# A two-layer hybrid trunk on one core: ScalarE copies, a group of weight rests and the last layer's end put in another order

## The chip, the cores and the metric

The kernel runs on one core of a Trainium2 chip. A core has TensorE (PE, with its weight loads shown as PEld), VectorE (DVE), ScalarE (ACT), GpSimd (POOL) and SyncE (SP, which here only issues DMAs). Each engine takes its instructions strictly in program order. The metric is device microseconds of one execution of the whole program. Three runs of the kernel before gave 1378.09 us in the median (1377.64 to 1379.01).

## The reference

```python
for i in range(DEPTH):                       # 2 layers; x is 256 x 1024, float32
    u = x @ w_in[i]                          # 512 pool columns, 512 values, 512 gates
    y_pool = pool_mixer(u_pool, ...)         # trailing-window means, grouped projection
    y_conv = conformer_conv(u_val, u_gate, ...)   # v = a*sigmoid(gate); 31 causal taps; norm; silu; @ w_pw
    x = layer_norm(ALPHA * x + concat([y_pool, y_conv]) @ w_out[i], ...)
    if i % 2 == 0: f = swiglu(x, ...)        # dense, 2816 hidden columns
    else:          f = moe_swiglu(x, ...)    # 8 experts of 3584 hidden columns, the top 2 of each token
    x = layer_norm(ALPHA * x + f, ...)
    x = x + sigmoid(x @ ple_gate_w[i]) * (p[i] @ ple_w[i])
```

## The kernel before

Tokens stand in two halves of 128, called h = 0 and 1. For every projection the activations are transposed (token columns, 8 tiles k of 128 features) and are the stationary operand; a weight tile of up to 512 columns streams past them into one PSUM bank.

Products are made in float32 precision out of a reduced format (fp32r). Activations and weights are each split into a high part H (a copy rounded to fp32r by ACT, L143 for weights and L317 for activations) and a rest L, the difference, by DVE (L158 and L318). One product of a k tile is then three matmuls: xH by wH (L344), xH by wL (L348) and xL by wH (L349). Weights named in `DIRECT` are not split: one full float32 matmul (L341) takes the unsplit activations `f` and the weight as it was loaded. Narrow experts (64 places) hold H and L of their tokens side by side and need two matmuls (L344, L346) and a product with the matrix `shift` that adds the two halves (L1045).

All weights pass through one ring of 19 slots of 8 KB per partition ("w"). `Weights` holds them in the order of use. `prepare(name, n)` and `get(i)` call `advance`, which emits the cast on ACT and the rest on DVE for each weight item up to the wanted one, and goes on ahead of need up to the item `W.cap`, as long as no more than `W.hl` slots hold split weights. Where such a call stands in the code is where its casts and rests stand in ACT's and DVE's queues. The same calls issue the loads on SP, a number of slots ahead. The code's order is the engines' order; nothing reorders it.

The places that the change touches, in order of time:

- Start: `shift` is filled from the identity in the constants `con` (L299), then ACT loads its sigmoid table (L313), then the two halves of x and the first weights are split.
- `mixer`: gate and value projections of the convolution group, `gate(b, h)` and `value(b, h)`, with 256 columns each; `diagonals(b)` writes 16 diagonal matrices on ACT (L497), which `conv(b)` multiplies on PE (L503). In layer 1 `late` transposes and splits the second half of x, which the layer before left over; it runs in the middle of `value(0, 0)`.
- `moe`, before the experts: norm, then for each half transposes and splits, the product with expert 0's first weights w1 (`p1`), the routing (logits `lg`, mask `msk`, positions, `select`), and the split of the second weights `w3e0_0` (L848).
- `experts`: 56 blocks of 512 hidden columns, each up by w1 and w3, down by w2; the last four blocks are narrow.
- The end of `moe` and `embed_gate`: `last(h)` adds half h of the last expert's output (`ps_sc`), the norm follows (`norm_begin`, `norm_apply`), `to_xT` transposes and splits 512 features at a time, `emit` makes products of the embedding (`ps_ple`), and the gate projection (`ps_gate`, weights `gate0`, `gate1`, each 512 columns) is combined and stored by 512 or, at the very end, 256 columns.

`acc` takes one of four PSUM banks in turn and `mmt` one of the four others. `keep_warm(n)` makes n products that nobody reads. POOL computes the inverse root of the norm.

Of the kernel before, what the change touches and what calls it, by code (L numbers as in the profile page):

```python
# [17 lines left out]
P = 128  # L18
# [3 lines left out]
KD = D // P  # L22
# [12 lines left out]
ND = len(DENSE_CHUNKS)  # L35
SLOTS = 19
HL_START, HL_PRE, HL_FIRST, HL_SECOND, HL_MOE = 8, 12, 8, 6, 10
DIRECT = ("pw0", "pw1", "wo00", "wo01")
DT = 23
MORE_AT = 53  # L40
WARM = 16
# [4 lines left out]
WU_EARLY = 2  # L46
# [5 lines left out]
EM = 3, 0  # L52
GL = 6
END = ((0, 256), (256, 256))
# [139 lines left out]
def trunk(ctx: ExitStack, tc: tile.TileContext, a: dict, out: bass.AP):  # L194
    nc = tc.nc
# [9 lines left out]
    def acc(name, k=None):  # L205

        if k is None:
            k = at[0] % 4
            at[0] += 1
        return pacc.tile([P, 512], F32, tag=f"acc{k}", name=name)  # L210
# [85 lines left out]
    H = P // 2  # L296
    shift = cp.tile([P, P], F32R, name="shift")
    nc.gpsimd.memset(shift[:, H:].bitcast(F32), 0.0)
    nc.scalar.copy(shift[:, :H], ident[:, H:])  # L299
    wr = tl("m2", [KD, NE])  # L300
    nc.gpsimd.dma_start(wr, a["router"])
    neghalf = cp.tile([P, 1], F32, name="neghalf")
# [19 lines left out]
    def new_xT(f=None):  # L322
        return [Split(tl(f"xH{h}", [KD, P], F32R), tl(f"xL{h}", [KD, P], F32R), None if f is None else f[:, h])
                for h in range(2)]
# [10 lines left out]
    def to_xT(dst, src, c):  # L335

        split_into(dst[:, 4 * c:4 * c + 4, :], transposes(src[:, c * 512:(c + 1) * 512], 4))
# [124 lines left out]
    def mixer(l, xT, xr, late, loads):  # L462
# [31 lines left out]
        def diagonals(b):  # L494
            for i in range(2):
                for k in range(TAPS - DT):
                    nc.scalar.activation(dg[:, i * 8 + k], ident, AF.Copy, scale=weight(2 * b + i, DT + k))  # L497
# [8 lines left out]
        def gate(b, h, between=None):  # L506
            pg = acc("ps_g")
            proj(W.names[f"wg{b}{l}"], pg, xT[h], free=h == 1, also=lambda k: k == GB and between and between())
            nc.scalar.activation(vb[b][h], pg[:, :256], AF.Sigmoid)

        def value(b, h, between=None):
            pv = acc("ps_v")
            proj(W.names[f"wv{b}{l}"], pv, xT[h], free=h == 1, also=lambda k: k == GB and between and between())
            nc.vector.tensor_mul(vb[b][h], pv[:, :256], vb[b][h])
# [3 lines left out]
            copy(vT[b][:, :, 32 + h * P:32 + (h + 1) * P], transposes(vb[b][h], 2))  # L518

        W.temps = TEMPS_MIX  # L520
        diagonals(0)

        gate(0, 0)
        if l == 0:
            gate(0, 1)
            value(0, 0)
        else:
            value(0, 0, late)
            gate(0, 1)
        W.prepare(f"wg1{l}")  # L530
        value(0, 1, lambda: turn(0, 0))
# [306 lines left out]
    def moe(l, xr, gb1, mix, project):  # L838
# [6 lines left out]
        sc = norm_begin(xr[1], mix[1], lambda: to_xT(xT[0], xr[0], 1))  # L845
        for c in range(2):
            norm_apply(gb1, xr[1], sc, c)
        W.prepare("w3e0_0", None)  # L848
        table(AF.Sigmoid)

        p1 = [acc("p1") for _ in range(2)]
# [13 lines left out]
        to_xT(xT[1], xr[1], 0)  # L865
        router(0, range(KD))
        to_xT(xT[1], xr[1], 1)
        W.hl = HL_SECOND
        routed = []

# [45 lines left out]
        last = experts(ranks, gates, xr, yacc, (selT, gsl, xg), lambda: hidden(g, 512, 0),  # L916
                       lambda: over(ci, beyond, gate, xr, yacc), end)
        gb, (ple, emit, _) = late["gains"], late["ple"]
        xT2 = new_xT()
        table(AF.Sigmoid)  # L920
        last(0)
        sc = [norm_begin(yacc[0], None)]
        W.prepare(f"gate0{l}", 2)
        emit(EM[0])
        for c in range(2):
            norm_apply(gb, yacc[0], sc[0], c)
        to_xT(xT2[0], yacc[0], 0)
        emit(EM[1])
        last(1)
        W.prepare(f"gate0{l}", 3)  # L930
        to_xT(xT2[0], yacc[0], 1)
        emit(4 - EM[0] - EM[1])
        sc.append(norm_begin(yacc[1], None))
        W.prepare(f"gate0{l}", 4)
        for c in range(2):
            norm_apply(gb, yacc[1], sc[1], c)
        W.prepare(f"gate1{l}", None)
        return xT2, yacc, lambda c: to_xT(xT2[1], yacc[1], c), ple

    def route(lg):  # L940
# [96 lines left out]
    def experts(ranks, gates, xr, yacc, nxt, first, more, end):  # L1037
# [9 lines left out]
        for i, (e, c) in enumerate(BLOCKS):  # L1047
# [11 lines left out]
            p1 = mmt("p1")  # L1059
            final = i == len(BLOCKS) - 1  # L1060
            if final:
                W.cap = W.names[f"w2e{prev[0]}_{prev[1]}"][1]
            both(f"w1e{e}_{c}", [p1], [xg])
            if made is not None:
                prev[3] = made()
# [23 lines left out]
            if final:  # L1089
                down(ids[:1], paccs, pgT, pc == 0, False, True)  # L1090
                if narrow:
                    fold(p3, lo[:, 1])
                    g = glu(s_, p3, 512, par, gsl)
                W.cap = W.names[f"w2e{e}_{c}"][-1] + 1
                W.hl = HL_PRE
                down(ids[1:], paccs, pgT, False, pc == FE - 1, True, 2)
            else:
                down(ids, paccs, pgT, pc == 0, pc == FE - 1, True)
                if narrow:
                    fold(p3, lo[:, 1])  # L1100
                    g = glu(s_, p3, 512, par, gsl)
# [36 lines left out]
    def embed_gate(l, xT, late, xr, ple, last):  # L1138

        xTn = None if last else new_xT()  # L1140

        def combine(h, c, ps, i=0, n=512):

            sg = tl(f"s{h}", [512])[:, i:i + n]
            cs = slice(c * 512 + i, c * 512 + i + n)
            nc.scalar.activation(sg, ps[:, :n], AF.Sigmoid)  # L1146
            nc.vector.tensor_mul(sg, sg, ple[:, h, cs])  # L1147
            nc.vector.tensor_add(xr[h][:, cs], sg, xr[h][:, cs])  # L1148
            if last:
                nc.sync.dma_start(out[h * P:(h + 1) * P, cs], xr[h][:, cs])  # L1150

        for c in range(2):
            ids = W.names[f"gate{c}{l}"]
            for h in range(2):
                if last and c and h:

                    for i, n in END:
                        ps = acc("ps_gate")
                        for k in range(KD):
                            mm(ps[:, :n], xT[h][:, k, :], W.get(ids[k // 2]), (ALL, k % 2, slice(i, i + n)),  # L1160
                               k == 0, k == KD - 1)
                        combine(h, c, ps, i, n)
                    continue
                ps = acc("ps_gate")
                proj(ids[:2], ps, xT[h], last=False, free=h == 1)
                if c == h == 0 and not last:
                    late()
                    W.prepare(f"gate1{l}")
                if c and h == 0 and not last:
                    to_xT(xTn[0], xr[0], 0)  # L1170

                def between(k):
                    if c == h == 0 and last and k == GL:
                        late(0)
                    if c and h and k == GK:
                        to_xT(xTn[0], xr[0], 1)
                proj(ids[2:], ps, xT[h], 4, first=False, free=h == 1, also=between)
                if c == h == 0 and last:
                    late(1)
                combine(h, c, ps)  # L1180
                if c and h == 0 and not last:
                    W.prepare(f"wg1{l + 1}")
            if c == 0 and not last:
                W.prepare(f"wv0{l + 1}")
        if not last:
            W.temps = TEMPS_MIX
            W.hl = HL_PRE
            W.prepare(f"wv1{l + 1}", None)
            W.prepare(f"wu{l + 1}", WU_EARLY)
        return xTn, lambda: [to_xT(xTn[1], xr[1], c) for c in range(2)]  # L1190

    warm = tl("cat", [512], mybir.dt.bfloat16)
# [4 lines left out]
    for h in range(2):  # L1197
        split_into(xT[h], xF[:, h])
        W.prepare("wg00" if h == 0 else "wv00")
    late = lambda: None  # L1200
    loads = mixer_loads(0)
    for l in range(L):
# [100 lines left out]
```

## Time and profile before

| what | value |
|---|---|
| median of three runs | 1378.09 us (1377.64 to 1379.01) |
| profiled execution, its own time | 1376.18 us |
| its span, first to last instruction | 1374.4 us |
| PE busy, matmuls | 1317.2 us (96%) x6314 |
| DVE busy | 1173.5 us (85%) |
| ACT busy | 921.8 us (67%) |
| rests of weights on DVE (L158) | 460, 891.8 us |
| casts of weights on ACT (L143) | 460, 750.8 us |
| read from HBM | 430.85 MB, 314 GB/s over the span |
| mean granted TensorE clock | 0.986 of full |

The span begins with the first instruction; the execution's own time is 1.8 us longer, and the median of the three runs another 1.9 us. PE's shares are high nearly everywhere, so a change in the order of work is read at the places where PE stands idle and at what ends that wait, with the name after the arrow in a row of the trace.

### The profile page before, as it was taken

What the parts mean: (1) busy time and instruction counts of PE and PEld (TensorE: products, weight loads), DVE (VectorE), ACT (ScalarE), POOL (GpSimd) and SP (SyncE); (2) the same over time, 40 slices, a digit from 0 to 9 for tenths busy, and PEclk for the clock granted to TensorE, in tenths of its full rate; (3) what the DMA queues carried; (4) which work ended last, traced back from release to release, by engine and by line L of the source; (5) the groups of instructions that cost most, each with busy time, mean ns of one, the idle gap of its engine ahead of it and who ended that gap; (6) DMA issues with size and microseconds to landing.
All of it is one profiled execution on the core that took longest, in us unless ns stands there. A gap on an engine that the chain in (4) does not pass through costs nothing. (4 is left out here: it accounts for less than half of the span.)

```text
span 1374.4 us, 17077 instructions
## 1 busy us (share of the span) xinstructions
PE 1317.2 (96%) x6314; PEld 1084.8 (79%) x6314; DVE 1173.5 (85%) x1102; ACT 921.8 (67%) x863; POOL 26.0 (2%) x33
## 2 busy tenths in 40 slices
PE   6999999999999999999999999999999999999777
PEld 5868888888967788878888878888887888888556
DVE  3987755466786989999999999999999999999885
ACT  5534544336333768887887887888787888898662
POOL 0000000010000200000000000000000000000000
PEclk8999999999998999999999999999999999999999
DMA  9436555526554499999999999999999999999850
GB/s 375 157 139 217 214 191 195 191 91 242 210 218 157 180 341 405 420 418 359 422 420 394 410 421 379 397 421 405 396 420 404 379 419 414 388 377 420 353 213 31
DMA packets 62172, 433.09 MB, mean 315 GB/s; under 512 B 6960, under 2 KB 7472, under 8 KB 11008
## 3 DMA queue, kind: packets, MB, share of 16 engines
q1 hardware_dynamic: 60336, 425.60, 78.5%
q0 software_dynamic: 1168, 4.23, 0.9%
q10 hardware_dynamic: 576, 2.10, 0.4%
q8 instruction: 51, 0.84, 0.2%
q14 instruction: 41, 0.34, 0.1%
HBM read 430.85 MB, written 1.05 MB: 314 GB/s over the span
## 5 line engine op out<-in xcount | busy, mean ns | idle before, releaser
L158 DVE TENSOR_TENSOR w<-w 128x2048 fp32r<-128x2048 f32 (+1 forms) x460 | 891.8, 1987 | 56.4 <-ACT w L143 49.8
L143 ACT CAST w<-w 128x2048 fp32r<-128x2048 f32 (+1 forms) x460 | 750.8, 1672 | 134.7 <-PE p L348 42.7
L344 PE MATMUL p<-w,xH 128*128 128x512 f32 (+1 forms) x1096 | 433.5, 396 | 9.5 <-ACT w L143 6.6
L349 PE MATMUL p<-w,xL 128*128 128x512 f32 (+1 forms) x648 | 250.9, 387 | 1.3 <-DVE xL L318 1.3
L348 PE MATMUL p<-w,xH 128*128 128x512 f32 (+1 forms) x648 | 250.2, 386 | 0.4 <-DVE w L158 0.4
L344 PEld LDWEIGHTS p<-w,xH 128*128 128x128 f32 x1096 | 207.6, 189 | 51.8 <-ACT w L143 7.0
L344 PE MATMUL y<-w,gH 128*128 128x512 f32 x448 | 176.2, 393 | 3.1 <-DVE gH L379 2.4
L346 PE MATMUL p<-w,xH 128*128 128x512 f32 x448 | 175.8, 392 | 0.0
L349 PEld LDWEIGHTS p<-w,xL 128*128 128x128 f32 x648 | 122.4, 189 | 26.7 <-DVE xL L318 1.8
L348 PEld LDWEIGHTS p<-w,xH 128*128 128x128 f32 x648 | 122.6, 189 | 24.6 <-DVE w L158 1.3
L344 PEld LDWEIGHTS y<-w,gH 128*128 128x128 f32 x448 | 84.6, 189 | 21.6 <-DVE gH L379 3.1
L346 PEld LDWEIGHTS p<-w,xH 128*128 128x128 f32 x448 | 85.0, 190 | 16.9
L346 PE MATMUL y<-w,gH 128*128 128x512 f32 x224 | 88.3, 394 | 1.9 <-DVE w L158 1.9
L349 PE MATMUL y<-w,gL 128*128 128x512 f32 x224 | 87.4, 390 | 1.2 <-DVE gL L318 1.2
L348 PE MATMUL y<-w,gH 128*128 128x512 f32 x224 | 87.3, 390 | 0.0
L484 DVE SCALAR_TENSOR_TENSOR yc<-w,vec,yc 128x256 f32<-128x256 f32 x176 | 70.4, 478 | 0.0
L645 ACT ACTIVATE s<-p 128x512 f32<-128x512 f32 (+1 forms) x69 | 41.2, 599 | 27.7 <-PE p L349 27.7
L318 DVE TENSOR_TENSOR gL<-tr,gH 128x512 fp32r<-128x512 f32 x38 | 25.7, 684 | 32.7 <-ACT gH L317 32.7
L346 PEld LDWEIGHTS y<-w,gH 128*128 128x128 f32 x224 | 42.6, 190 | 11.0 <-DVE w L158 2.3
L317 ACT CAST gH<-tr 128x512 fp32r<-128x512 f32 x38 | 21.9, 587 | 43.6 <-PE tr L332 43.0
L349 PEld LDWEIGHTS y<-w,gL 128*128 128x128 f32 x224 | 42.0, 188 | 10.4 <-DVE gL L318 1.6
L348 PEld LDWEIGHTS y<-w,gH 128*128 128x128 f32 x224 | 42.1, 188 | 9.0
(223 smaller groups left out, 1415.9 us busy)
## 6 DMA issues: line engine op xcount, KB each, us to landing
w<-in_exp_w SPq DMA_DIRECT2D x336, 1024.0 KB, 8.7
w<-in_dense_w SPq DMA_DIRECT2D x33, 1024.0 KB, 5.0
w<-in_w_out SPq DMA_DIRECT2D x8, 1024.0 KB, 6.4
w<-in_ple_gate_w SPq DMA_DIRECT2D x8, 1024.0 KB, 5.1
w<-in_w_gv SPq DMA_DIRECT2D x6, 1024.0 KB, 7.2
w<-in_w_u SPq DMA_DIRECT2D x4, 1024.0 KB, 10.2
w<-in_w_gv SPq DMA_DIRECT2D x4, 512.0 KB, 7.3
w<-in_w_small SPq DMA_DIRECT2D x2, 1024.0 KB, 9.1
```

What stands on the lines that cost most here:

```text
L143: nc.scalar.copy(h, w)
L158: engine.tensor_tensor(l, w, h.bitcast(F32), op=ALU.subtract)
L317: nc.scalar.copy(dst.h, src)
L318: nc.vector.tensor_sub(dst.l, src, dst.h.bitcast(F32))
L344: nc.tensor.matmul(ps, x.h, wh, start=start, stop=False)
L346: nc.tensor.matmul(ps, x.h, wl, start=False, stop=stop)
L348: nc.tensor.matmul(ps, x.h, wl, start=False, stop=False)
L349: nc.tensor.matmul(ps, x.l, wh, start=False, stop=stop)
L484: nc.vector.scalar_tensor_tensor(yc[:, ct], src, weight(ct, t), yc[:, ct], op0=ALU.mult, op1=ALU.add)
L645: nc.scalar.activation(s_[:, :nf], p1[:, :nf], AF.Silu)
```

## The change

Seven edits, in order of time:

1. The copy into `shift` is issued after both halves of x and the first weights are split.
2. In layer 1, `diagonals(0)` is issued after `value(0, 0)` with its `late` part, not before `gate(0, 0)`.
3. `W.prepare("w3e0_0", None)` is issued after both transposes of half 1.
4. In the last expert block `W.cap` is raised to the block's own w2 at its start.
5. `gate11` (the second 512 columns of the last gate) is added to `DIRECT`, and layer 1's last `xT2` gets an unsplit part `f`, one more ring slot and one more ACT copy per `to_xT`.
6. After `last(0)` the norm, transposes, weights and embedding products come in another order: the first half is transposed and split before the second is normed, and `keep_warm(8)` stands before it.
7. The last layer's gate runs half by half and not column by column, with half 1's transposes inside the second projection; the last 512 columns are two pieces of 256, now direct.

```diff
-DIRECT = ("pw0", "pw1", "wo00", "wo01")
+DIRECT = ("pw0", "pw1", "wo00", "wo01", "gate11")
...
     nc.gpsimd.memset(shift[:, H:].bitcast(F32), 0.0)
-    nc.scalar.copy(shift[:, :H], ident[:, H:])
...
-        diagonals(0)
+        if l == 0:
+            diagonals(0)
...
             value(0, 0, late)
+            diagonals(0)
             gate(0, 1)
...
-        W.prepare("w3e0_0", None)
         table(AF.Sigmoid)
...
         to_xT(xT[1], xr[1], 1)
+        W.prepare("w3e0_0", None)
         W.hl = HL_SECOND
...
-        xT2 = new_xT()
+        xT2 = new_xT(W.temp([2, KD, P]))
         table(AF.Sigmoid)
         last(0)
         sc = [norm_begin(yacc[0], None)]
+        W.prepare(f"gate0{l}", 1)
+        emit(EM[0])
+        keep_warm(8)
+        norm_apply(gb, yacc[0], sc[0], 0)
+        to_xT(xT2[0], yacc[0], 0)
+        norm_apply(gb, yacc[0], sc[0], 1)
         W.prepare(f"gate0{l}", 2)
-        emit(EM[0])
-        for c in range(2):
-            norm_apply(gb, yacc[0], sc[0], c)
-        to_xT(xT2[0], yacc[0], 0)
+        to_xT(xT2[0], yacc[0], 1)
         emit(EM[1])
         last(1)
         W.prepare(f"gate0{l}", 3)
-        to_xT(xT2[0], yacc[0], 1)
...
-        W.prepare(f"gate1{l}", None)
+        W.prepare(f"gate1{l}")
...
             if final:
-                W.cap = W.names[f"w2e{prev[0]}_{prev[1]}"][1]
+                W.cap = W.names[f"w2e{e}_{c}"][-1] + 1
...
-                W.cap = W.names[f"w2e{e}_{c}"][-1] + 1
                 W.hl = HL_PRE
...
+        def pieces(h, c):
+            for i, n in END:
+                ps = acc("ps_gate")
+                for k in range(KD):
+                    it = W.get(ids[k * len(ids) // KD])
+                    mm(ps[:, :n], xT[h][:, k, :], it, (ALL, k % it["k"], slice(i, i + n)), k == 0, k == KD - 1)
+                combine(h, c, ps, i, n)
+
+        if last:
+            for h in range(2):
+                for c in range(2):
+                    ids = W.names[f"gate{c}{l}"]
+                    if c and h:
+                        pieces(h, c)
+                        continue
+                    ps = acc("ps_gate")
+                    n = len(ids) // 2
+                    proj(ids[:n], ps, xT[h], last=False)
+                    proj(ids[n:], ps, xT[h], 4, first=False, also=lambda k: k == GL and c and late(0))
+                    if c:
+                        late(1)
+                    combine(h, c, ps)
+            return None, None
...
+    nc.scalar.copy(shift[:, :H], ident[:, H:])
     late = lambda: None
     loads = mixer_loads(0)
```

ACT's queue at the program's start, before. `xH_141` and `xH_143` are the high parts of the two halves of x, `w<-w` the casts of the first weights, the 16 ACTIVATE the diagonal matrices.

```order
L299 ACT_TABLE_LOAD
L299 CAST shift<-con 128x64
L313 ACT_TABLE_LOAD
L313 ACTIVATE dummy<-neghalf 128x1
L317 CAST xH_141<-w 128x1024
L143 CAST w<-w 128x1024 x2
L317 CAST xH_143<-w 128x1024
L143 CAST w<-w 128x1024 x2
L497 ACTIVATE w<-con,vec 128x128 x16
```

The same queue after (line numbers have moved by one or more).

```order
L312 ACT_TABLE_LOAD
L312 ACTIVATE dummy<-neghalf 128x1
L316 CAST xH_140<-w 128x1024
L143 CAST w<-w 128x1024 x2
L316 CAST xH_142<-w 128x1024
L143 CAST w<-w 128x1024 x2
L1213 CAST shift<-con 128x64
L496 ACTIVATE w<-con,vec 128x128 x16
```

The copy that reads `con` has gone from the first place to the place ahead of the diagonal matrices, and one table load is gone.

DVE's queue between the norm of half 1 and the routing, before: the norm of `xr_97`, the four rests of `w3e0_0`, the rests of half 1's activations, the logits.

```order
L413 SCALAR_TENSOR_TENSOR xr_97<-xr_97,mv,w 128x512
L414 SCALAR_TENSOR_TENSOR xr_97<-xr_97,rs,w 128x512
L158 TENSOR_TENSOR w<-w 128x1024 x4
L318 TENSOR_TENSOR xL_3185<-tr,xH_3184 128x512 x2
L876 COPY lg<-ps_r 128x8
L877 TENSOR_TENSOR lg<-lg,ps_r 128x8
```

After:

```order
L412 SCALAR_TENSOR_TENSOR xr_97<-xr_97,mv,w 128x512
L413 SCALAR_TENSOR_TENSOR xr_97<-xr_97,rs,w 128x512
L317 TENSOR_TENSOR xL_3185<-tr,xH_3184 128x512 x2
L158 TENSOR_TENSOR w<-w 128x1024 x4
L877 COPY lg<-ps_r 128x8
L878 TENSOR_TENSOR lg<-lg,ps_r 128x8
```

The four rests now stand between the activations' rests and the logits; on ACT the four casts have moved in the same way behind the casts of half 1 (L317).

DVE's queue around the last expert blocks' products, before: `g` is a block's gated hidden tile, `gH` its transposed and split form.

```order
L654 SCALAR_TENSOR_TENSOR g_13266<-p_13204,gsl_9137,s_13235 128x512
L158 TENSOR_TENSOR w<-w 128x2048
L379 TENSOR_TENSOR gH_13295<-tr,gH_13295 128x4x64
L654 SCALAR_TENSOR_TENSOR g_13334<-p_13304,gsl_9137,s_13323 128x512
L158 TENSOR_TENSOR w<-w 128x2048 x3
L379 TENSOR_TENSOR gH_13358<-tr,gH_13358 128x4x64
```

After:

```order
L655 SCALAR_TENSOR_TENSOR g_13266<-p_13204,gsl_9137,s_13235 128x512
L158 TENSOR_TENSOR w<-w 128x2048 x2
L378 TENSOR_TENSOR gH_13301<-tr,gH_13301 128x4x64
L158 TENSOR_TENSOR w<-w 128x2048 x2
L655 SCALAR_TENSOR_TENSOR g_13352<-p_13310,gsl_9137,s_13341 128x512
L378 TENSOR_TENSOR gH_13362<-tr,gH_13362 128x4x64
```

All four rests of the two last w2 now stand ahead of the last block's `g`; three stood behind it.

## Rows read from the trace of the kernel before

**Rows 1.** Stages: length; busy time by engine (count); PEclk, DMA share, GB/s

```profile
15.00:20.00 5.00, 2.81 (x11) 2.52 (x12) 4.64 (x5) 5.00 (x7) 0.00 (x0) 0.50 1.01 424
...
420.00:450.00 30.00, 27.18 (x145) 23.23 (x144) 17.85 (x49) 11.13 (x17) 0.92 (x1) 0.83 0.48 172
...
900.00:1290.00 390.00, 378.32 (x1758) 311.36 (x1756) 383.72 (x254) 324.38 (x246) 0.62 (x1) 1.00 0.99 402
```

**Rows 2.** Timeline, ACT at the start: start, length, instruction [idle before, releaser]

```profile
12.63 0.24 ACT L299 CAST shift<-con 128x64 fp32r<-128x64 f32 x1 [10.62 <-DMA con<-in_con]
...
15.23 1.99 ACT L143 CAST w<-w 128x1024 fp32r<-128x1024 f32 x2
```

**Rows 3.** Timeline, PE: the first product, and conv(0) of layer 0

```profile
16.32 0.58 PE L344 MATMUL ps_g<-w,xH 128*128 128x256 f32 x1 [9.67 <-ACT w L143]
...
34.41 7.08 PE L503 MATMUL ps_c<-w 128*128 128x256 f32 x32
```

**Rows 4.** Timeline, SP: issues of wv00 in two pieces, of wu0

```profile
2.58 1.03 SPq L114 DMA_DIRECT2D w<-in_w_gv  x2
...
8.17 1.62 SPq L114 DMA_DIRECT2D w<-in_w_u  x2
```

**Rows 5.** DMA issues: count, KB, us to landing; second piece of wv00, second wu0

```profile
w<-in_w_gv SPq DMA_DIRECT2D x1, 512.0 KB, 8.9
...
w<-in_w_u SPq DMA_DIRECT2D x1, 1024.0 KB, 13.5
```

**Rows 6.** Timeline, start of layer 1: ACT, then PE

```profile
330.73 4.79 ACT L497 ACTIVATE w<-con,vec 128x128 f32<-128x128 f32 x16
...
336.31 0.58 PE L344 MATMUL ps_g<-w,xH 128*128 128x256 f32 x1 [3.28 <-ACT xH L317]
...
340.81 0.28 PE L344 MATMUL ps_v<-w,xH 128*128 128x256 f32 x1
```

**Rows 7.** Timeline ahead of the experts: DVE, then PE

```profile
427.32 4.62 DVE L158 TENSOR_TENSOR w<-w 128x1024 fp32r<-128x1024 f32 x4
...
437.92 0.17 DVE L876 COPY lg<-ps_r 128x8 f32<-128x8 f32 x1 [4.51 <-PE ps_r L861]
...
440.23 0.17 DVE L966 TENSOR_SCALAR msk<-rank 128x16 f32<-128x16 f32 x1
...
430.52 0.50 PE L344 MATMUL p<-w,xH 128*128 128x512 f32 x1 [1.48 <-ACT xH L317]
...
442.46 0.28 PE L977 MATMUL ps_pos<-msk,con 128*128 128x8 f32 x2
...
444.97 0.38 PE L767 MATMUL ps_sel<-con,m 128*128 128x128 f32 x2
```

**Rows 8.** Timeline, last expert block: DVE's g, PE's last down products

```profile
1316.48 0.75 DVE L654 SCALAR_TENSOR_TENSOR g<-p,gsl,s 128x512 f32<-128x512 f32 x1 [4.24 <-PE p L1045]
1317.15 6.69 DVE L158 TENSOR_TENSOR w<-w 128x2048 fp32r<-128x2048 f32 x3
...
1324.22 0.50 PE L344 MATMUL y<-w,gH 128*128 128x512 f32 x1 [1.06 <-DVE gH L379]
```

**Rows 9.** Page, part 5: activations' rests and casts; busy, mean ns | idle before

```profile
L318 DVE TENSOR_TENSOR gL<-tr,gH 128x512 fp32r<-128x512 f32 x38 | 25.7, 684 | 32.7 <-ACT gH L317 32.7
...
L317 ACT CAST gH<-tr 128x512 fp32r<-128x512 f32 x38 | 21.9, 587 | 43.6 <-PE tr L332 43.0
```

**Rows 10.** Timeline, the end and the direct products of layer 0

```profile
1336.40 0.66 PE L332 MATMUL tr<-con,w 128*128 128x128 f32 x4 [2.10 <-DVE w L414]
...
1352.26 0.51 PE L349 MATMUL ps_gate<-w,xL 128*128 128x512 f32 x1 [4.02 <-DVE xL L318]
...
1370.38 0.38 ACT L1146 ACTIVATE s<-ps_gate 128x256 f32<-128x256 f32 x1 [2.49 <-PE ps_gate L349]
...
72.67 7.03 PE L341 MATMUL ps_o<-w,cat 128*128 128x512 f32 x16
```

**Rows 11.** Chain that ended last: start, length, one split gate matmul

```profile
1363.23 0.23 PE ps_gate L344
```

More of the change, by code (lines that the diff above doesn't have):

```diff
@@ L1154, in embed_gate @@
             for h in range(2):
[L1155 to L1163, printed above, removed]
                 ps = acc("ps_gate")
                 proj(ids[:2], ps, xT[h], last=False, free=h == 1)
-                if c == h == 0 and not last:
+                if c == h == 0:
                     late()
                     W.prepare(f"gate1{l}")
-                if c and h == 0 and not last:
+                if c and h == 0:
                     to_xT(xTn[0], xr[0], 0)
                 def between(k):
-                    if c == h == 0 and last and k == GL:
-                        late(0)
                     if c and h and k == GK:
@@ L1177, in embed_gate @@
                 proj(ids[2:], ps, xT[h], 4, first=False, free=h == 1, also=between)
-                if c == h == 0 and last:
-                    late(1)
                 combine(h, c, ps)
-                if c and h == 0 and not last:
+                if c and h == 0:
                     W.prepare(f"wg1{l + 1}")
-            if c == 0 and not last:
+            if c == 0:
                 W.prepare(f"wv0{l + 1}")
[L1185 to L1189, printed above, removed]
+        W.temps = TEMPS_MIX
+        W.hl = HL_PRE
+        W.prepare(f"wv1{l + 1}", None)
+        W.prepare(f"wu{l + 1}", WU_EARLY)
         return xTn, lambda: [to_xT(xTn[1], xr[1], c) for c in range(2)]
```

## The prediction

> **What bounds the kernel now.** I read the table of stages first, then, on each engine, the idle time that stands in front of an instruction and the name that ended it, and last the chain that ended the program. The stages say that TensorE is the bound almost throughout: in the expert stage it is idle for 390.00 - 378.32 = 11.7 us only, with DVE at 383.72 and the DMA share at 0.99 close behind it [rows 1]. A microsecond won ahead of such a stage moves the stage as a whole. So what counts is where PE stands still. There are five such places, and the change touches each.
>
> At the start ACT waits 10.62 us for the constants, and everything else on ACT stands behind that copy [rows 2]; PE waits 9.67 us for its first product and begins at 16.32 [rows 3]. At the start of layer 1 PE waits 3.28 us for an activation cast, which stands behind 16 diagonal matrices of 4.79 us in all [rows 6]. Ahead of the experts PE waits 1.48 us for such a cast again, this time behind casts of w3, and its clock is low afterwards: the granted clock of that stage is 0.83 in the mean [rows 1, 7]. In the last expert block DVE idles 4.24 us and then does three rests, 6.69 us, for which PE waits [rows 8]. In the last gate PE waits 4.02 us for xL behind four more rests [rows 10].
>
> **Start (edit 1).** The copy costs 0.24 us and drags a second table load along; what counts is its wait. Behind the edit ACT works off x and wg00 as they land, ahead of wv00 in the queue. The second piece of wv00 is the last to come: issued at about 3.1 (second of the two issues from 2.58) and 8.9 us under way, 12.0 [rows 4, 5]. Cast 1.0 (half of 1.99 [rows 2]), rest 1.15 (a quarter of 4.62 [rows 7]): value products can begin at about 14.3. The 48 products of both gates come before that: a matmul of 256 columns takes 0.12, half of the 0.23 that 512 take [rows 11], so 5.7 us. Another 5.7 for the value products and 0.5 for transposes between them: PE is through with them at 20.6. Beside that runs ACT's chain: wv00's cast until 13.0, the moved copy (con landed at 12.6) 0.24, diagonals 4.79 as in [rows 6], two sigmoids of 0.4 (256 columns, by the 0.59 for 512 [rows 9]), casts of wg1 at 19.8 and 20.8, rests 1.15 behind each: 21.0 and 22.1. gate(1,0), 24 products with one wait for a transpose in the middle, ends at 24.4, and conv(0) begins there, not at 34.41 [rows 3]. That is **10.0 us**. Late next are the loads of wu: the second, issued by about 9.5, lands 13.5 later [rows 4, 5], 23.0, and ACT asks for it at 24.8, a cover of 1.8 us. Bounds: 6.5, if PE runs the four groups at the lower clock level as it did between 15 and 20 (0.50 [rows 1]) and ends them at 24.9 and gate(1,0) at 27.9; 11 from above.
>
> **Layer 1 (edit 2).** PE could go on at 336.31 - 3.28 = 333.0. Without the 4.79 us ahead of them the casts end at about 332.3; xL follows behind DVE's rests, which costs PE about 0.5. 24 products at 0.12 and that wait end at 336.4, where the trace has 340.81 [rows 6]: **4.4 us**, 3.28 of it the wait and the rest products that no longer run slowly. The diagonals now stand ahead of one sigmoid, which they delay to 337.1; the next that needs it is a DVE product behind 24 more matmuls, 339.2, so this is hidden, and conv(0) comes later still. Bounds: 3.3 (the wait alone) and 4.8.
>
> **Ahead of the experts (edit 3).** ACT casts half 1 as it is transposed, and PE, free since 430.52 - 1.48 = 429.0 [rows 7], goes on at once. But the four rests (4.62) now stand on DVE between xL and the logits. Casts of half 1 end at 429.65, xL at 430.35, the fourth rest, behind a cast chain of four times 1.0, at 435.2, the second copy of the logits starts at 435.7 instead of 437.92. The mask came 440.23 - 437.92 = 2.3 later; PE had by then reached the positions only at 442.46 [rows 7]. Now PE gets there at 435 and waits for the mask until 438.2. Five small products (1.0) and six of 0.23 follow: 440.7 for ps_sel against 444.97, **4.2 us**. So the next late thing is the logits behind the rests. Bounds: 1.5, if the clock falls in that new wait and the transposes and gathers behind it run at half speed; 5.
>
> **Last expert block (edit 4).** DVE does the two rests in its 4.24 us of idle time that stood ahead of g, and one of them runs over. One rest is 2.23 (a third of 6.69). g waits for the two, 1319.0 instead of 1316.48, plus transposes 0.66, cast and gH's rest about 0.9: PE's last down products begin at about 1321.4 instead of 1324.22 [rows 8]: **2.8 us**; 0 to 4.2.
>
> **The end (edits 5 to 7).** In the old clock of the trace, so without the 2.8: one rest leaves the place ahead of the norm, and eight unused products, 8 x 0.23 = 1.8, fit into PE's wait of 2.10 ahead of the transposes [rows 10], so these begin at 1336.1, 0.3 earlier. Uncovered they would cost 1.8. Then DVE, which used to go on with the second half, waits: transposes 0.66, cast 0.59, xL 0.68 [rows 9, 10], two steps of the norm of about 0.7 each: 1339.4. Second transposes 0.66, then the scatter's four matmuls (0.9) and six of the embedding (1.4): the gate starts at 1342.4. From there PE has 48 split matmuls at 0.23, 11.0, and 16 direct products. A direct product is two entries of the trace: 8 of them take 7.03, 0.88 each [rows 10], so 14.1 for the sixteen, where three split matmuls would be 11.0: **3.1 us more**. With 0.9 for transposes and 0.6 for the last rest of gate0 the last matmul ends at 1369.0 against 1370.38 [rows 10]. The four rests of 4.6 and the 4.02 wait pay for the slower products: **1.3 us** remain; -3 to +3.
>
> The row on ACT's cast and DVE's rest shows the two taking turns on one PSUM tile: DVE waits for ACT in all of its 32.7 us of idle time there [rows 9]. The Trainium skill's page "PSUM — Partial Sum Buffer" (section "PSUM bank collisions raise a hardware error ⚠️") says that two engines must not even read one bank at the same time. By that rule the new unsplit copy on ACT, which only reads what DVE reads too, stands behind xL; no run here shows it yet. I count its 0.4 in the 0.6 above; without the rule the end would be 1368.6.
>
> **Sum.** 10.0 + 4.4 + 4.2 + 2.8 + 1.3 = 22.7. The profiled execution took 1376.18, of it 1374.4 its span: 1353.5. The median of the runs shown lies 1.9 higher: **1355.4 us**.
>
> **Rivals.**
> *The clock falls in the new pauses.* PE now idles for a short while three times: before 8 us at the start, 3.2 us at the mask, and around the last block. For it: in the trace products ran at the lower level after each of the waits at the start and ahead of the experts [rows 1]. Against: the new pauses are shorter or broken by products. Price: start 3.5, experts 2.7, the end 1 (its products at half speed for two), 7.2: 1362.6. The skill's page "TensorE: Matmul & The Clock Gate" (section "HAM oscillation — how this bites in real kernels") describes it: pauses between bursts bring the clock down, and each fall is paid again. Chance 0.2.
> *The start is hidden behind the loads.* The first loads saturate the DMA engines (share 1.01 [rows 1]), and landings take 8.9 to 13.5 us [rows 5]; if wg1 and wu came as much as that difference, 4.6, later than they do now, the 10.0 would shrink to 5.4: 1360.0. Against: nothing is issued earlier than before, and the loads that are needed next had landed by 23. Chance 0.12.
> *The experts are bound by their transfers, and it gets slower.* With the DMA share at 0.99 [rows 1] the stage could end when its last weights land, whatever is won ahead of it or in its last block; then only the end's own balance is left, the 3.1 of the direct products with the gain of the order used up by the later start: 1381.2. It decides from the point where PE's waits for weights eat up more than the 22 us won. Against: PE idles 11.7 us in 390, DVE's busy time is nearly as full, and the loads are issued as slots come free, so that the stream moves along with PE. Chance 0.04.
> *It doesn't do what it says*: casts that move could wait for ring slots instead, and the time stay within the noise. 0.02.
>
> **How the numbers follow.** The forecast 0.62, its own range 1351 to 1359 from the bounds of the start and the end. The range of 8 in 10 reaches down to the upper bounds of two terms (11 and +3, 2.7 more than counted, and half of the others') and up past the clock's rival: 1351 to 1365. A difference below 0.2% (2.8 us) can't be told from none here. Faster: 0.62 + 0.20 + 0.12 = 0.94. Same 0.02, the change that does not do what it says; slower, by the transfers, 0.04.
>
> **What the changed profile will show.** Right: PE's first product at 7 to 9 us, conv(0) near 24; no wait over 1 us and a full clock at the start of layer 1; a wait for the mask of about 3 us on PE ahead of the experts, ps_sel some 18.6 us earlier than before; DVE without its 4.24 us gap; 16 direct gate products of 0.88 (the last eight in two pieces). Wrong: a granted clock of 0.5 anywhere between 8 and 20 us (3.5 us); new waits of PE for weights in the expert stage, or its length changed by more than 2 us; PE waiting for xL or f in the last gate for over 2 us. The forecast falls if conv(0) begins later than 29 or the expert stage takes up what came before it.

## The result, and the profile after

The changed kernel took 1354.31 us (median of four runs, 1353.94 to 1354.62) against 1378.2 for the kernel before: a ratio of 0.9826, interval 0.9809 to 0.9843. The forecast was 1355.4 in a range of 1351 to 1365. The profiled execution took 1354.37, of it 1352.6 its span, 21.8 less than before; the sum of the prediction had 22.7.

In the table each place is one instruction of TensorE or ACT, with its start before and after (line numbers are one lower or a few higher than before); "step" is what was won since the row above.

| place | before | after | won so far | step | forecast |
|---|---|---|---|---|---|
| conv(0) of layer 0 | 34.41 | 23.32 | 11.1 | 11.1 | 10.0 |
| second value group, layer 1 | 340.81 | 325.35 | 15.5 | 4.4 | 4.4 |
| ps_sel ahead of the experts | 444.97 | 426.24 | 18.7 | 3.3 | 4.2 |
| ps_s behind the gather | 449.20 | 431.31 | 17.9 | -0.8 | 0 |
| last down products | 1324.22 | 1303.17 | 21.05 | 3.2 | 2.8 |
| last activation | 1370.38 | 1348.54 | 21.8 | 0.8 | 1.3 |

The start, as a timeline of ACT and then of PE (start, length, instruction, idle before it and what ended it), answers to [rows 2, 3]. ACT casts x at 4.88, and the moved copy, now at 12.41, waits for nothing:

```profile
4.88 1.04 ACT L316 CAST xH<-w 128x1024 fp32r<-128x1024 f32 x1 [2.65 <-DMA w<-in_xT]
6.16 1.04 ACT L143 CAST w<-w 128x1024 fp32r<-128x1024 f32 x1 [0.23 <-DMA w<-in_w_gv]
...
11.46 1.05 ACT L143 CAST w<-w 128x1024 fp32r<-128x1024 f32 x1 [0.20 <-DMA w<-in_w_gv]
12.41 0.24 ACT L1213 CAST shift<-con 128x64 fp32r<-128x64 f32 x1
...
7.25 0.38 PE L343 MATMUL ps_g<-w,xH 128*128 128x256 f32 x1 [0.70 <-ACT w L143]
...
23.32 7.07 PE L502 MATMUL ps_c<-w 128*128 128x256 f32 x32
```

Four stretches of the changed kernel, in the columns of [rows 1]. The first holds the start's gates and values, now at the full level of the clock (1.00). The third is the expert stage of [rows 1], shifted by the 18 us won ahead of it: PE's busy time there is 378.42 where it was 378.32, so the stage took up nothing. The second and the fourth ran at the lower level (0.51), and the sum did not have them:

```profile
8.00:24.00 16.00, 15.49 (x127) 15.40 (x128) 10.74 (x11) 14.01 (x31) 0.00 (x0) 1.00 1.02 414
424.60:428.00 3.40, 3.40 (x14) 2.92 (x13) 0.81 (x6) 0.86 (x2) 0.00 (x0) 0.51 0.50 171
882.00:1272.00 390.00, 378.42 (x1758) 311.42 (x1756) 383.75 (x254) 324.49 (x246) 0.62 (x1) 1.00 1.00 402
1319.00:1322.30 3.30, 3.30 (x10) 2.57 (x9) 2.79 (x5) 2.12 (x3) 0.00 (x0) 0.51 0.02 5
```

Layer 1, timeline, answers to [rows 6]: the diagonal matrices take their 4.79 us behind the casts, and PE's wait of 3.28 is down to 0.43, for xL.

```profile
321.07 4.79 ACT L496 ACTIVATE w<-con,vec 128x128 f32<-128x128 f32 x16
...
322.61 0.39 PE L348 MATMUL ps_g<-w,xL 128*128 128x256 f32 x1 [0.43 <-DVE xL L317]
...
325.35 0.28 PE L343 MATMUL ps_v<-w,xH 128*128 128x256 f32 x1
```

Ahead of the experts, DVE and then PE, answers to [rows 7]: the four rests end at 419.99, the logits follow, and PE waits 3.11 us for the mask.

```profile
415.44 4.63 DVE L158 TENSOR_TENSOR w<-w 128x1024 fp32r<-128x1024 f32 x4 [0.25 <-ACT w L143]
419.99 0.16 DVE L877 COPY lg<-ps_r 128x8 f32<-128x8 f32 x1
...
422.57 0.17 DVE L969 TENSOR_SCALAR msk<-rank 128x16 f32<-128x16 f32 x1
...
422.89 0.36 PE L980 MATMUL ps_pos<-msk,con 128*128 128x8 f32 x2 [3.11 <-DVE msk L969]
...
426.24 0.63 PE L768 MATMUL ps_sel<-con,m 128*128 128x128 f32 x2
...
431.31 1.02 PE L893 MATMUL ps_s<-s,m 128*128 128x512 f32 x2
```

The last expert block, DVE and PE, answers to [rows 8]: the two rests stand ahead of g, without DVE's gap of 4.24.

```profile
1296.39 4.48 DVE L158 TENSOR_TENSOR w<-w 128x2048 fp32r<-128x2048 f32 x2
1300.80 0.74 DVE L655 SCALAR_TENSOR_TENSOR g<-p,gsl,s 128x512 f32<-128x512 f32 x1
...
1303.17 0.50 PE L343 MATMUL y<-w,gH 128*128 128x512 f32 x1 [0.92 <-DVE gH L378]
```

The end, PE and then ACT, answers to [rows 10]. The unused products run right up to the first transposes; the second transposes wait 2.94 for the norm; the direct products, 0.44 for each entry, follow without a wait:

```profile
1313.12 1.90 PE L308 MATMUL warm<-con 128*128 128x512 bf16 x8
1314.86 0.60 PE L331 MATMUL tr<-con,w 128*128 128x128 f32 x4
1318.39 0.67 PE L331 MATMUL tr<-con,w 128*128 128x128 f32 x4 [2.94 <-DVE w L413]
...
1328.22 6.17 PE L340 MATMUL ps_gate<-w 128*128 128x512 f32 x14
...
1336.20 0.59 ACT L319 COPY w<-tr 128x512 f32<-128x512 f32 x1 [0.76 <-DVE xL L317]
...
1348.54 0.38 ACT L1148 ACTIVATE s<-ps_gate 128x256 f32<-128x256 f32 x1 [3.07 <-PE ps_gate L340]
```

### The profile page after: what moved, and what is told of

It is laid out like the page before. It is cut to its first block, busy times and chain, and to the rows that moved or that the text cites. A ratio compares the mean times of both kernels' runs of the same rounds, so it can differ in the third digit from the quotient of the medians.

```text
span 1352.6 us, 17041 instructions
## 1 busy us (share of the span) xinstructions
PE 1313.0 (97%) x6298; PEld 1078.3 (80%) x6298; DVE 1170.0 (87%) x1098; ACT 919.8 (68%) x862; POOL 25.9 (2%) x33
## 5 line engine op out<-in xcount | busy, mean ns | idle before, releaser
L317 DVE TENSOR_TENSOR gL<-tr,gH 128x512 fp32r<-128x512 f32 x38 | 25.6, 683 | 32.7 <-ACT gH L316 32.7
```

Of the source, the lines that this page charges most:

```text
L317: nc.vector.tensor_sub(dst.l, src, dst.h.bitcast(F32))
```

## The experiments

My theory: five local gains, each set by the wait named for it, which pass through the stages behind them whole. Its rivals: the stages behind take something back, or the edits need each other. First each part alone in the kernel before. Every ratio is to the kernel before on the same chip. "The end" is the time from the last down products to the last activation.

**The shift copy alone.**

```
-    nc.scalar.copy(shift[:, :H], ident[:, H:])
     wr = tl("m2", [KD, NE])
...
         W.prepare("wg00" if h == 0 else "wv00")
+    nc.scalar.copy(shift[:, :H], ident[:, H:])
```

> The kernel before with one edit, the copy of the shift matrix behind the first activations and weights. My theory (ACT's wait for the constants held up all casts, and with them PE's first product and its clock, and what is won there reaches the end whole): conv(0) of layer 0 begins at 23.3 instead of 34.41, no stretch at 0.5 before 30 us, and the kernel is 11.1 us faster than before, 1367.1. Rival A (part of the gain is taken back by the loads in the expert stage, which no longer has the other edits' room): 8 us or less, with PE's idle time in the stage grown by 3 or more. Rival B (the start needs the other edits too): conv(0) later than 25.

1367.55 us against 1377.43, ratio 0.9930 (0.9916 to 0.9944): 9.9 us, and the interval holds the 11.1 that I expected. conv(0) began at 23.89. Of its 10.5 us, 9.1 were left at the last down products: 0.5 was lost in layer 1 up to the second value group, 0.7 from there to the positions and 0.2 in the expert stage. So the gain passes nearly whole; the start needs no other edit, and rivals A and B fall.

**The diagonal matrices alone.**

```
-        diagonals(0)
+        if l == 0:
+            diagonals(0)
...
             value(0, 0, late)
+            diagonals(0)
```

> The kernel before with one edit, the diagonal matrices of layer 1 behind the first value group. My theory (PE's 3.28 us wait was for a cast behind the 16 matrices, and the lower clock behind it belongs to it): the second value group of layer 1 begins 4.4 us earlier, and 4.1 to 4.4 reach the end: 1373.9. Rival (the granted clock there hangs on the changed start, not on the wait): the wait goes, but a stretch at 0.5 near 336 stays; 3.3 or less: 1375.

1373.31, ratio 0.9965 (0.9951 to 0.9978): 4.1 us. From conv(0) of layer 0 to the second value group of layer 1 it took 301.99 instead of 306.40, 4.4 less. The wait and the low clock went together (PE's timeline, then a stretch in the columns of [rows 1]), although the start was as before; so the rival falls:

```profile
334.00 0.39 PE L349 MATMUL ps_g<-w,xL 128*128 128x256 f32 x1 [0.43 <-DVE xL L318]
...
332.00:340.00 8.00, 7.57 (x64) 7.36 (x63) 2.87 (x5) 6.92 (x22) 0.00 (x0) 1.00 0.68 236
```

**w3's first casts and rests alone.**

```
-        W.prepare("w3e0_0", None)
         table(AF.Sigmoid)
...
         to_xT(xT[1], xr[1], 1)
+        W.prepare("w3e0_0", None)
```

> The kernel before with one edit, the casts and rests of the first w3 behind the second half's activations. My theory: PE no longer waits for the activations ahead of the experts but 3 us for the mask; ps_sel comes 3.5 us earlier, a fall of the clock behind the mask's wait takes 0.8 of it, and 2.7 reach the end: 1375.5. Rival A (the clock stays low from the first wait on as before, since only the order changes): 1 us or less: 1377.2. Rival B (the wait for the mask is paid in full and nothing is left): no change, 1378.2.

1376.1, ratio 0.9986 (0.9977 to 0.9995): 1.3 us, about half of what I expected, with an interval that holds 2.7 as well as the 1 of rival A; rival B falls. The trace decides for my theory: from the first conv of layer 1, ps_sel came 3.8 earlier and ps_s 2.7. Of the 2.7, this execution had lost 0.5 ahead of that conv, where the slow products of layer 1 lasted longer, and lost 0.8 in the old end, which took 47.0 us against 46.2. The low stretch moved from ahead of the positions to behind them (a stretch of the kernel before, then PE and a stretch of this one):

```profile
432.60:441.70 9.10, 9.10 (x29) 7.87 (x30) 3.94 (x22) 2.18 (x4) 0.00 (x0) 0.50 0.76 290
...
438.59 0.36 PE L977 MATMUL ps_pos<-msk,con 128*128 128x8 f32 x2 [3.10 <-DVE msk L966]
...
440.50:443.90 3.40, 3.40 (x15) 3.00 (x14) 0.60 (x5) 0.86 (x2) 0.00 (x0) 0.50 0.49 145
```

**The limit in the last block alone.**

```
             if final:
-                W.cap = W.names[f"w2e{prev[0]}_{prev[1]}"][1]
+                W.cap = W.names[f"w2e{e}_{c}"][-1] + 1
...
-                W.cap = W.names[f"w2e{e}_{c}"][-1] + 1
                 W.hl = HL_PRE
```

> The kernel before with one edit, the limit on how far weights are made ready raised at the head of the last expert block. My theory (DVE does two rests in its idle time ahead of g, and PE's last down products come that much sooner): DVE's 4.24 us gap is gone, the last down products begin 3.1 us earlier, 3.1 at the end: 1375.1. Rival (in the old order of the end the norm's first rests are still late, and the wait ahead of the transposes of the end grows by what is won): the down products come 3.1 earlier but under 1.5 reaches the end: 1377.

1373.96, ratio 0.9974 (0.9965 to 0.9984): 3.5 us. From ps_s to the last down products 871.71 instead of 875.02, 3.3 less. PE waits the same 2.10 and 4.02 in the old end; neither grew by the gain, and the rival falls.

**The end alone** (edits 5 to 7: the order shown ahead of the prediction, the unused products, gate11 direct).

```
-DIRECT = ("pw0", "pw1", "wo00", "wo01")
+DIRECT = ("pw0", "pw1", "wo00", "wo01", "gate11")
...
+        keep_warm(8)
         norm_apply(gb, yacc[0], sc[0], 0)
```

> The kernel before with the end's edits alone (order of the last layer's norm and gate, eight unused products, gate11 direct). Theory A (as the trace of the changed kernel puts it, from the last down products to the last activation 0.8 us are won): 0.8 us faster than before, 1376.6. Theory B (the four edits tried so far alone gave 9.9 + 4.1 + 1.3 + 3.5 = 18.8 of 23.1, and the rest belongs to the end): 4.3 us faster, 1373.1, since the new end no longer loses to a lower clock what the old one loses in some executions. Theory C (the new order needs the rests that edit 4 has done early): no faster than before, 1378 or more.

1376.51 against 1378.7, ratio 0.9987 (0.9978 to 0.9996): 2.2 us, between A and B. The interval, 0.6 to 3.0 us, holds A's 0.8, which this trace shows again (45.4 us for the end against 46.2), and neither B's 4.3 nor C. The five ratios multiply to 0.9843; the whole change had 0.9826, and 0.9839 in a second comparison (below, up to 0.9852). The parts add up within what can be measured.

What the end is worth depends on which old end it is compared with. The old order took 46.2, 46.6, 49.1, 47.0, 46.6 and 46.6 us in six kernels, the new one with all its parts 45.4, 45.4, 45.3 and 45.3 in four. The longest, 49.1, is that of the kernel with the diagonal matrices alone. Three stretches ran at the lower level there, the first of which begins 5.7 us ahead of the last down products. This agrees with the reason that theory B gives: the mean granted clock of that execution was 0.981, and it was 0.980 to 0.982 in 11 of the 15 executions of the kernel before behind this ratio, but 0.984 to 0.986 in all 11 of the kernel with the new end. No run shows where those executions of the kernel before lose their time.

```profile
1313.80:1323.80 10.00, 8.56 (x21) 6.49 (x22) 8.25 (x7) 4.40 (x5) 0.00 (x0) 0.50 0.50 187
1334.20:1337.40 3.20, 3.20 (x12) 2.63 (x11) 3.17 (x6) 1.91 (x3) 0.00 (x0) 0.50 0.02 5
1347.90:1354.50 6.60, 4.80 (x11) 3.79 (x12) 3.63 (x6) 0.00 (x0) 0.00 (x0) 0.50 0.10 40
```

**The constants first.** The shift copy stays where it was; its load goes ahead of x and the weights.

```
+    con = cp.tile([P, NC_], F32, name="con")
+    nc.sync.dma_start(con, a["con"])
     xF = W.temp([2, KD, P])
     nc.sync.dma_start(xF[:, 0], a["xT"][0])
...
-    con = cp.tile([P, NC_], F32, name="con")
-    nc.sync.dma_start(con, a["con"])
```

> The kernel before with the shift copy where it was and the load of the constants put first in the queue, ahead of x and the weights. My theory (it was ACT's wait for the constants, and not the copy's place or its table load, that held up the start): ACT waits under 4 us, x and the weights land 0.6 later than in the changed kernel, conv(0) of layer 0 begins at 24.0 to 24.5, and the kernel is 10 us faster than before, a ratio of 0.9927. Rival (the copy and the second table load ahead of the first activation cost of their own): conv(0) at 25.5 or later, 8.5 us.

1370.38 against 1377.45, ratio 0.9947 (0.9934 to 0.9961): 7.1 us; conv(0) at 27.9. My number failed and the mechanism held: with 1.31 us left of its wait for the constants, ACT is through with the copy at 3.6. But what ACT waits for then is not the copy or the table load, as the rival has it, but x and wg00, which land 0.8 and 2.3 later than in the changed kernel. PE's wait for the cast is 2.42 instead of 0.70, and the products behind it ran at the lower level (ACT, PE, then the stretch):

```profile
3.32 0.24 ACT L299 CAST shift<-con 128x64 fp32r<-128x64 f32 x1 [1.31 <-DMA con<-in_con]
...
8.45 1.04 ACT L143 CAST w<-w 128x1024 fp32r<-128x1024 f32 x1 [1.76 <-DMA w<-in_w_gv]
...
9.54 0.58 PE L344 MATMUL ps_g<-w,xH 128*128 128x256 f32 x1 [2.42 <-ACT w L143]
...
9.50:16.00 6.50, 5.78 (x25) 5.49 (x26) 6.12 (x5) 5.58 (x10) 0.00 (x0) 0.50 1.04 422
```

Up to the first value product the two gates take 9.3 us here and 7.0 in the changed kernel; with the first product 2.3 later this makes the 4.6 by which conv(0) is late. The prediction's lower bound for the start also had conv(0) at 27.9, but that they agree is chance: that bound had all four groups slow and the landings as they were.

**Without the unused products** (the changed kernel from here on).

```
-        keep_warm(8)
```

> The changed kernel without the eight unused products in the wait for the first norm. My theory (they fill a wait of 2 us and keep the clock from falling there, without being on the path themselves): the first transposes begin within 0.3 us of the same time, but a stretch at 0.5 stands ahead of the first gate products or is longer, and the kernel is 0.5 to 1.5 us slower, 1355.3. Rival (the clock falls anyway in the next wait, of 2.94 us, and the products do nothing): the same within 0.3, 1354.3. Other side (they delay the transposes): 0.5 faster, 1353.8.

1355.0 against 1378.7, ratio 0.9825 (0.9812 to 0.9839), the changed kernel's own. The first transposes came 11.03 after the last down products instead of 11.69: the eight products were on the path, by 0.66, and the end took 44.8 instead of 45.4. So in the trace the other side holds, by an amount that the times can't show, and my theory falls. The clock fell at the same place as with them (PE, then the stretch):

```profile
1316.21 0.66 PE L331 MATMUL tr<-con,w 128*128 128x128 f32 x4 [0.96 <-DVE w L413]
...
1320.70:1324.00 3.30, 3.30 (x9) 2.62 (x8) 2.84 (x5) 1.89 (x3) 0.00 (x0) 0.51 0.02 5
```

**gate11 split again.**

```
-DIRECT = ("pw0", "pw1", "wo00", "wo01", "gate11")
+DIRECT = ("pw0", "pw1", "wo00", "wo01")
```

> The changed kernel with gate11 split as before (four casts and four rests again, three products for one). The prediction's count (direct costs PE 3.1 us more, the rests and the wait behind them cost 4.4): 1.3 or so slower than the changed kernel, 1355.6, with PE waiting over 1 us for a rest or for xL in the last gate. Rival (in the new order DVE is free for the rests, between 1329.8 and 1335, so that they are hidden and the direct products' extra time is all that is left): 1.5 to 2 us faster, 1352.5, no wait over 1 us.

1355.75, ratio 0.9834 (0.9819 to 0.9850): can't be told from the changed kernel. PE does wait for a rest, as counted, so the rival's "no wait over 1 us" falls, but the end took 44.7 instead of 45.4: the rests cost no more than the direct products do (DVE, then PE):

```profile
1330.68 4.62 DVE L158 TENSOR_TENSOR w<-w 128x1024 fp32r<-128x1024 f32 x4
...
1331.95 0.50 PE L347 MATMUL ps_gate<-w,xH 128*128 128x512 f32 x1 [1.62 <-DVE w L158]
```

**Both waits filled** (fill(n): n unused products into one PSUM tile).

```
                 gate, msk = routed
+                fill(10)
...
         to_xT(xT2[0], yacc[0], 0)
+        fill(10)
```

> The changed kernel with ten more unused products in each of two waits: ahead of the positions (3.11 us, for the mask) and ahead of the second transposes of the end (2.94 us). My theory (the two waits bring the clock to 0.5 behind them, and this costs 0.8 ahead of the experts and 1.6 at the end): both stretches at 0.5 go, ps_s comes 0.8 earlier after the positions and the first gate product 1.6 earlier after the transposes; 2.4 us faster than the changed kernel, 1351.9. Rival A (the clock falls all the same, since unused products do not hold it): no change, 1354.3. Rival B (the products run into the work behind them): up to 1 us slower, 1355.3.

1354.56, ratio 0.9825 (0.9812 to 0.9839): no gain. The two places differ (PE, then three stretches). Ahead of the experts the wait left was 0.94 and the clock fell all the same, a little later: rival A. At the end it stayed at 1.00 and the gate began 1.6 sooner after the transposes: my theory, and not the spread between executions: in the six traces of the new end with that wait left open the gate began 4.31 to 4.35 us after the second transposes, here 2.75. But then PE waited for gate0's fourth rest, which the slow start had hidden, and 1.0 of the end was left.

```profile
423.57 0.36 PE L988 MATMUL ps_pos<-msk,con 128*128 128x8 f32 x2 [0.94 <-DVE msk L977]
...
1327.16 0.50 PE L353 MATMUL ps_gate<-w,xH 128*128 128x512 f32 x1 [0.40 <-DVE w L158]
...
426.00:429.30 3.30, 3.30 (x16) 3.00 (x16) 0.16 (x1) 0.86 (x2) 0.00 (x0) 0.53 0.52 151
1319.50:1323.00 3.50, 3.46 (x18) 2.97 (x19) 3.11 (x4) 2.05 (x5) 0.00 (x0) 1.00 0.00 0
```

**Two rests behind the selection, and a version that fits the waits.** On one chip: the changed kernel again, the same with the first two edits below, and with all of them.

```
-        W.prepare("w3e0_0", None)
+        W.prepare("w3e0_0", 2)
...
         sel, cc = select(0, posm, gate, 0, 0)
+        W.prepare("w3e0_0", None)
...
-        keep_warm(8)
...
         to_xT(xT2[0], yacc[0], 0)
+        emit(4 - EM[0] - EM[1])
+        fill(5)
...
         W.prepare(f"gate0{l}", 3)
-        emit(4 - EM[0] - EM[1])
-        sc.append(norm_begin(yacc[1], None))
         W.prepare(f"gate0{l}", 4)
+        sc.append(norm_begin(yacc[1], None))
```

> The changed kernel itself, again, to stand beside its variants on one chip. All theories: a ratio to before of 0.9826 as measured, 1354.3 where before takes 1378.2; from the positions to ps_s 8.4 us or, where the low clock lasts longer, up to 10.

1354.45 against 1377.45, ratio 0.9839 (0.9826 to 0.9852); 8.4 from the positions to ps_s.

> The changed kernel with one more edit, two of w3's first four rests behind the selection. My theory (the four rests ahead of the logits cost PE the wait for the mask, 3.11): the wait 0.8, 2.3 us faster than the changed kernel, and 0.8 more if the clock stays up. Rival (the moved casts delay the activation of the first expert's rows, and the gather waits): the wait is shorter but ps_s comes no sooner, no change.

1352.41, ratio 0.9819 (0.9805 to 0.9832): 2.0 us less, with intervals that overlap slightly. The wait for the mask is 0.83, and ps_s came 2.3 earlier after the first conv of layer 1; the clock fell around the selection, from 423.1 on.

> The changed kernel with five more edits: two of w3's first four rests stand behind the selection and not ahead of the logits; the eight unused products are gone; the last six products of the embedding stand in the wait ahead of the second transposes of the end, with five unused products behind them; gate0's fourth rest goes ahead of the second norm's statistics. My theory (the two waits of 3.11 and 2.94 us can be filled or shortened, and the clock then stays up): the wait for the mask 0.8 instead of 3.11, ps_s 2.3 to 3.1 earlier after the first conv of layer 1; the last activation 42.8 after the last down products instead of 45.37; 4.9 to 5.7 us faster than the changed kernel. Rival (the clock falls ahead of the experts all the same, and gate0's rests take the end's gain): 2.3 and under 1, some 3 us. Other side (the moved casts stand in the way of the first gather): not faster.

1349.85, ratio 0.9797 (0.9783 to 0.9810): 4.6 us below the changed kernel, and the intervals don't touch. The end took 42.8 as expected; what each of its edits gave was not tried alone. Ahead of the experts the low stretch came early, before the positions, and ate the 2.2 of the wait there; from the positions to ps_s it took 6.7 at the full level. So the expected 0.8 for a clock that stays up was not had. And no pause stood ahead of this fall: PE was busy for all of the 16 us from 400 to 416, the last 6 of which are shown, and had begun on the router's products (ps_r). The rows are PE of the kernel with two edits, then PE and stretches of the one with all.

```profile
420.75 0.36 PE L981 MATMUL ps_pos<-msk,con 128*128 128x8 f32 x2 [0.83 <-DVE msk L970]
```

```profile
1316.29 0.63 PE L337 MATMUL tr<-con,w 128*128 128x128 f32 x4 [0.46 <-DVE w L419]
...
1321.48 0.50 PE L353 MATMUL ps_gate<-w,xH 128*128 128x512 f32 x1 [0.68 <-DVE w L158]
...
410.00:416.00 6.00, 6.00 (x44) 5.50 (x43) 3.69 (x7) 2.22 (x4) 0.48 (x1) 1.00 0.55 195
416.00:422.80 6.80, 6.80 (x21) 5.67 (x20) 5.70 (x23) 4.13 (x6) 0.00 (x0) 0.50 0.57 206
423.30:430.00 6.70, 6.70 (x55) 6.39 (x54) 4.09 (x12) 1.73 (x4) 0.00 (x0) 1.00 0.17 39
1316.00:1320.00 4.00, 3.71 (x19) 3.17 (x20) 3.16 (x5) 2.70 (x4) 0.00 (x0) 1.00 0.02 6
```

## Why the prediction was right, and where not

*The number* came closer than its terms. The lower clock took 3.1 us that the sum did not have (1.7 ahead of the experts, 1.4 at the end); 1.1 more at the start, 0.4 more in the last block and 0.8 less in the gate offset 2.2 of them, which leaves 21.8 for 22.7. The 1.9 us added for the median did not apply: the changed kernel's profiled execution, 1354.37, lies at its median, while that of the kernel before lay 1.9 below its own. So the medians are 23.9 apart and the two profiled executions 21.8, and the forecast missed by only 1.1 because two errors, 0.9 and 1.9, went opposite ways; that is luck. Of the clock's rival, 7.2, the 3.1 came and the 3.5 of the start did not.

*Start, 10.0; it was 11.1.* The mechanism was right: the copy alone gives 9.9, and putting the load first instead removes the same wait. The value products began at 14.24, counted at 14.3, though behind the last gate product and not behind wv00's rest. One link did not bind: wv00's second piece was cast from 11.46, where I had it land at 12.0, and the casts of wg1 began at 17.8 instead of 18.8, so that PE, through at 20.2, did not wait for wg1's rest until 21.0. Part of the 1.1 is spread: in the eight traces with the copy moved conv(0) began between 23.28 and 24.01.

*Layer 1, 4.4; it was 4.4,* in the change and alone; the lower clock belonged to the wait, as counted.

*Ahead of the experts, 4.2; it was 3.3, and 2.4 at ps_s.* The new wait for the mask was counted at 3.2 and is 3.11. The step that failed is "five small products (1.0) and six of 0.23 follow": PE came out of the wait and its clock fell, so that positions to ps_s took 8.4 instead of 6.7. That is the place that the clock's rival named, with 2.7; it cost 1.7 here and 3.1 to 3.2 in two of the variants. The filled wait shows that not PE's pause at the mask alone sets it, and in the fitted kernel the clock fell with no pause ahead of it.

*Last block, 2.8; it was 3.2,* and 3.3 alone.

*The end, 1.3; it was 0.8,* by two errors that offset each other in part. The second transposes were due at 1339.4 in the times of before, which is 1318.35 with the 21.05 won by then, and came at 1318.39. The time of the first ones was right too (1336.1 is 1315.05; they came at 1314.86), but the eight unused products do not "fit into PE's wait of 2.10": that wait had a rest of 1.2 in it, which the same edit takes away, and 0.96 is left, so that the products themselves set that time and cost 0.66. Behind the second transposes the clock fell, and ten products took 4.0 us instead of 2.3: the gate began 1.4 late. The step that failed here is "the gate starts at 1342.4". On the other side the gate took 25.8 and not 26.6, as no rest of gate0 had to be waited for. The direct products gain nothing over the split ones within what can be measured.

The copies of f wait 0.76 us for DVE's xL on the same tile each time. The Trainium skill's page "PSUM — Partial Sum Buffer" (section "PSUM bank collisions raise a hardware error ⚠️") has two readers of one bank kept apart; the trace agrees. PE waits for none of the copies, so the 0.4 that the prediction counted for one, for which it names no row, was not paid.

Of the other rivals, "the start is hidden behind the loads" falls with conv(0) at 23.32. "The experts are bound by their transfers" falls with the stage's busy time, 378.42 beside 378.32, and with five parts each of which shows at the end.

Left open: what brings the clock down ahead of the experts in each of these kernels, at one place or another. A filled wait did not stop it, and it came without a wait too. In all of them PE does the router's products (ps_r, 0.11 us each) ahead of it; no run changed these, so whether they matter is not shown.

## What to carry to other kernels

On an engine that works in order, look for the first instruction that waits for something late and is needed late: what it holds up is worth more than what it costs (0.24 us of copy, 11 us of start). Where an edit takes an instruction out of a wait, subtract it from the wait before something else is put in. And count each new wait of TensorE twice, once as time and once as the slower products that may follow; but look at the granted clock where there is no wait as well, since it fell there too.

## What the runs showed that was not expected

The low stretch ahead of the experts moves and changes its length between kernels that do the same there: 424.6 to 428 in the changed one and 423 to 430 in two variants of its end; from 423.1 with two rests behind the selection, but 416 to 422.8 in the fitted one, which does the same up to the experts. From positions to ps_s that is 8.4, 9.8 to 10.0, 8.4 and 6.7 us.

Unused products held the clock at the end (ten in a wait of 2.94: 1.00 instead of 0.51) and not ahead of the experts (ten in a wait of 3.11: still 0.53). Eight of them one wait earlier changed nothing behind the next.

232.5 KB put first in the queue delayed x by 0.8 us and the first weights by 2.3: at the 414 GB/s of the start's stretch the bytes alone take 0.6 us (an estimate), so the order of the loads cost more than their bytes.
